# A decoder block's feed-forward part: rows for four operand sums fetched one part earlier, and half of one inner product's weight differences made in later products

## The chip, the cores and the metric

The kernel runs on one core of one Trainium2 chip. The metric is the device time of one execution in microseconds (us); the time of a version is the median of its runs. A profile shows one execution, with the busy time of each engine: PE (TensorE, the matrix multiplies), DVE (VectorE), ACT (ScalarE), POOL (GpSimd) and SP (SyncE, which here only issues DMAs, in the order of its own instruction list).

## The reference, cut to what matters

One decoder layer: a mixer of pooling and attention, then a feed-forward part with the square of a ReLU, in float32, 2048 rows, width 1024, inner width 4096. The change is in the feed-forward part alone (the last three lines before the final norm):

```python
h = h + einsum('bse,ed->bsd', mixed, w_out)
hn2 = rmsnorm(h, norm2_g)
up = einsum('bsd,df->bsf', hn2, w_up)
act = square(relu(up))
h = h + einsum('bsf,fd->bsd', act, w_down)
return rmsnorm(h, final_g)
```

## The kernel before

Every float32 operand is split into a high and a low part, and a product is done as three matmuls on 128x128 weights and 128x512 rows. The split takes one ACT copy (line L146) and one DVE subtract (L147). Products are arranged in the way of Strassen: a block product is seven smaller products P1 to P7 on sums and differences of operand blocks.

**up()** computes the first matrix product in 32 columns, numbered (q, m): q is the first or second half of the rows, m one of 16 column blocks of `w_up`. A column is its seven products, twelve matmuls each (L1082, into the accumulators pX, pY and pZ), so 84 matmuls. The scheduler that lays out the program sets the order of the instructions on each engine, and it may put products of neighbouring columns next to each other. After a product, `post` does the work on its result: after P7 a DVE add (L1032) reads the accumulator pZ, and the twelve matmuls of P3, which go on accumulating in that same pZ, wait for it. `post` also stores the sums (L1003), 256 KB each.

The second half of the rows (q = 1) needs sums of its own operand blocks. They are made by `sums_second(n, part)` for n = 0 to 3, during the columns q = 0, m = 2 to 5: part 0 at product P2 of the column, part 1 at P5, part 2 at P4. A part calls `normed_of(h, i)`, which loads a 256 KB row block `hn` from `hs` by SP (L955) and scales it in place on DVE (L956). Then follow the adds (L951) and the stores (L950). DVE works in the order of its list, so an instruction that waits for `hn` holds up all behind it.

**down()** computes the second matrix product in seven products, one after the other: P1, P6, P7, then P4, P5 and P2, each of which is itself done by seven inner products, and at last P3. A step of P1, P6 or P7 is 48 matmuls (L1422): one 512 KB weight block `wr` (loaded at L1142, split into `wd`) and two 512 KB row blocks `ar` (loaded from `sd` at L1197, split into `ad`), one for each half of the rows. The eight steps of a product take the blocks in the order `TURN` = 3, 7, 2, 6, 1, 5, 0, 4. An inner step of P4, P5 or P2 is 12 matmuls (L1249).

The inner products of P4, P5 and P2 need differences of weight blocks. `inner_weights(i, kk, t)` makes them from a pair of blocks kk and kk + 4: four DVE subtracts of 128x512 (L1137) and four 256 KB stores (L1138). For P2 this is done during P1: `more_weights` loads block `w_down[2, kk]` once more for each of the eight steps. That is eight loads, sixteen subtracts and sixteen stores.

Loads by SP go through one queue with eight completion semaphores used in turn. A load or a store on SP therefore waits for the eighth one before it.

Of the kernel before, what the change touches and what calls it, by code (L numbers as in the profile page):

```python
# [46 lines left out]
def hymba_block(ctx: ExitStack, tc: tile.TileContext, xT, gains, w_in, pool_w, w_out, w_up, w_down, out):  # L47
    nc = tc.nc
# [84 lines left out]
    hs = [dram.tile([KD, P, T], F32, name=f"hs{j}") for j in range(NT)]  # L133
# [685 lines left out]
    def root_last(i, ss, where=None, tag="px"):  # L819
        y = inv_root(mean_squares([ss], D, where, tag), nc.gpsimd)  # L820
        nc.gpsimd.tensor_copy(yrlast[:, i, 0], y)
        nc.gpsimd.tensor_tensor(yrlast[:, i, 1], y, yrlast[:, i, 0].bitcast(F32), ALU.subtract)
# [18 lines left out]
    A11, A12, A22, S1, S2, S3, S4 = range(7)  # L841
    PAIRS = ((0, 1), (3, 2))
# [18 lines left out]
    def up(pools, more):  # L861
# [3 lines left out]
        cols = [(q, m + x * (NM // 2)) for q in range(2) for m in range(NM // 2)[::(1, -1)[q]] for x in range(2)]  # L865
# [78 lines left out]
        SUMS, second = ("P2", "P5", "P4"), {}  # L944

        def sums_second(n, part):

            c, k = n // 2, n % 2
            new = lambda name: avp.tile([P, T], F32, tag="av", name=name)
            keep = lambda i, t: nc.sync.dma_start(su[1][i][c][:, k], t)  # L950
            add = lambda to, x, y, op: nc.vector.tensor_tensor(to, x, y, op)  # L951

            def normed_of(h, i):
                t, j = new("hn"), PAIRS[1][h]
                nc.sync.dma_start(t, hs[j][i])  # L955
                nc.vector.scalar_tensor_tensor(t, t, g2[:, i:i + 1], rlast[:, j - 2], op0=ALU.mult, op1=ALU.mult)  # L956
                return t

            if part == 0:
                second["a21"], a22 = normed_of(1, n), normed_of(1, 4 + n)  # L960
                second["s1"] = new("hs1")
                add(second["s1"], second["a21"], a22, ALU.add)
                keep(A22, a22)
                keep(S1, second["s1"])
            elif part == 1:
                a11, a21, s1 = normed_of(0, n), second["a21"], second["s1"]
                add(a21, a11, a21, ALU.subtract)
                second["s2"] = new("hs2")
                add(second["s2"], s1, a11, ALU.subtract)
                keep(A11, a11)  # L970
                keep(S3, a21)
                keep(S2, second["s2"])
            else:
                a12, s4 = normed_of(0, 4 + n), new("hs4")
                keep(A12, a12)
                add(s4, a12, second["s2"], ALU.subtract)
                keep(S4, s4)
# [90 lines left out]
        for g, (q, m, s) in enumerate(slots):  # L1068
            while lefts and lefts[0][0] <= g + LA:
                make_left(*lefts.pop(0)[1:])  # L1070
            if q == 0 and 2 <= m < 6 and s in SUMS:
                sums_second(m - 2, SUMS.index(s))
            if q == 0 and (m in (1, 6, 7) or m >= NM // 2 and m % (NM // 2) not in (2, 3, 4, 5)) and s in SUMS:
                next(first_weights, None)
            bank, first, last = what[s][2:]
            if first:
                ps[q, m, bank] = psu.tile([P, T], F32, tag=bank, name="p" + bank)
            t, w = ps[q, m, bank], ops.pop(g)
            for c in range(G):
                a = left_ops[q, s][c // 2]  # L1080
                for x, (wx, ax) in enumerate(((0, 0), (0, 1), (1, 0))):
                    nc.tensor.matmul(t, w[:, wx, c], a[:, ax, c % 2], start=first and c == 0 and x == 0,  # L1082
                                     stop=last and c == G - 1 and x == 2, skip_group_check=True)
            post(q, m, s)
            if g == 1:
                root_last(1, sslast, psu, "R")
            elif g in (6, 10):
                pr, i = psu.tile([P, T], F32, tag="R", name="pr"), g // 10
                spread(pr, yrlast[:, i])
                nc.scalar.activation(rlast[:, i], pr, AF.Copy)  # L1090
            if g + UA < len(slots):
                make_weights(g + UA)
                q2, m2, s2 = slots[g + UA]
                n = cols.index((q2, m2)) + 2
                if s2 == "P3" and n < 2 * NM:
                    load(*cols[n])

    def down(pools):
# [9 lines left out]
            else:  # L1108
                steps += [(n, i, kk, (0, 1)) for kk in range(8)]
        steps += [("P3", S4, kk, (q,)) for q in range(2) for kk in range(8)]  # L1110
        made, turns = {}, {"ar": -2, "ad": 0}

        def row(shape, kind, tag, **kw):
            early, late_ = {"ar": rs, "ad": s8}[tag]
# [14 lines left out]
        def inner_weights(i, kk, t):  # L1129

            if kk < 4:
                tops[i] = t
                return
            b, k = {(x, y): half(w, y) for x, w in enumerate((tops.pop(i), t)) for y in range(2)}, kk - 4
            for to, x, y, p in (((0, 0), (0, 1), (0, 0), "P5"), ((0, 1), (1, 1), (0, 1), "P7"),
                                ((1, 1), (1, 1), (0, 0), "P6"), ((1, 0), (1, 0), (1, 1), "P4")):
                nc.vector.tensor_tensor(b[to], b[x], b[y], ALU.subtract)  # L1137
                nc.sync.dma_start(wi[i][p][k // 2][:, 2 * (k % 2):2 * (k % 2) + 2], b[to])  # L1138

        def blk(i, kk, where=None):  # L1140
            t = (where or rt).tile([P, 4, 256], F32, tag="wr", name="wr")
            nc.sync.dma_start(t, w_down[i, kk] if isinstance(i, int) else td[int(i[1]) - 1][kk])  # L1142
            return t
# [4 lines left out]

        def more_weights(n, kk, w):

            if n == "P1":
                inner_weights(A12, kk, blk(2, kk))
            elif n == "P6":
                minus(blk(2, kk, rtx), w)
                nc.sync.dma_start(td[1][kk], w)
            elif n == "P7":
                inner_weights(A22, kk, blk("t2", kk))

        def make_inner(n, p, kk):

            i, kp = SPLIT[n], kk // 2
            if kk % 2 == 0:
                if p in wi[i]:
                    w = rt.tile([P, 4, 256], F32, tag="wr", name="wq")
                    nc.sync.dma_start(w, wi[i][p][kp])
                else:
                    w = quarter(source[n], kp, *{"P1": (0, 0), "P2": (1, 0), "P3": (1, 1)}[p])
                t = made["inner"] = t8.tile([P, 2, 4, 256], F32R, tag="wd", name="wd", align_bytes=256)
            r = row([P, 2, T], F32, "ar")
            nc.sync.dma_start(r, {"P1": sd[0][i][kk], "P2": sd[0][i][kk + 4], "P4": sd[1][i][kk + 4]}[p]  # L1170
                              if p in ("P1", "P2", "P4") else sdi[i][("P5", "P6", "P7", "P3").index(p)][kk])
            if kk % 2 == 0:
                split((t[:, 0], t[:, 1]), w)
            a = row([P, 2, 2, T], F32R, "ad", align_bytes=256)
            split((a[:, 0], a[:, 1]), r)
            return made["inner"], a

        def make(g):
            n, i, kk, qs_ = steps[g]
            if qs_ is None:  # L1180
                made[g] = make_inner(n, i, kk)
                return
            if n != "P3":
                kk = TURN[kk]
            b11, b12, b21, b22 = range(4)
            if n == "P1":
                w = blk(b11, kk)
            elif n == "P6":
                w = minus(blk(b22, kk), blk("t1", kk))
            elif n == "P7":  # L1190
                w = minus(blk(b22, kk), blk(b12, kk))
            else:
                w = blk(b22, kk)
            rows = {q: row([P, 2, T], F32, "ar") for q in qs_}
            for q in qs_:
                with tc.issue_after(last[0].ins) if n == "P1" and last[0] else nullcontext():
                    last[0] = nc.sync.dma_start(rows[q], sd[q][i][kk])  # L1197
            t = t8.tile([P, 2, 4, 256], F32R, tag="wd", name="wd", align_bytes=256)
            split((t[:, 0], t[:, 1]), w)
            left_ = {}  # L1200
            for q in qs_:
                left_[q] = row([P, 2, 2, T], F32R, "ad", align_bytes=256)
                last[1] = split((left_[q][:, 0], left_[q][:, 1]), rows[q])
            while late and n != "P1":
                late.pop(0)()
            late.append(lambda: more_weights(n, kk, w))
            made[g] = t, left_
# [200 lines left out]
        for g, (n_, i, kk, qs_) in enumerate(steps):  # L1408
            t, left_ = made.pop(g)
# [204 lines left out]
```

## Time and profile before

| | |
|---|---|
| median of 3 runs | 1913.87 us (1913.1 to 1915.24) |
| the profiled execution, its own time | 1917.71 us |
| its span, first to last instruction | 1915.9 us |
| PE busy in the span | 1891.8 us (99%) |
| up(), 2688 matmuls of 128x512 | about 698 to 1312 us |
| down(), products P1, P6, P7 (1152 matmuls) | 1312.12 to 1575.41 us |
| down(), products P4, P5, P2 (1008 matmuls) | 1575.41 to 1804.87 us |

Times inside the span count from its first instruction. A row of a timeline gives the start, the duration, the engine, the line of the kernel, the operation, the output and the input, how many instructions it stands for, and in brackets the idle time before it with what ended it. A run of twelve matmuls shows 2.88 us, of which the last part overlaps with the next run: the next one starts 2.72 us later. A row of the chain of waits gives a start, a duration and who held the chain then. In a table by windows each engine has its busy time (with its instructions in brackets), then come the granted clock, the share of the 16 DMA engines' time and the rate in GB/s.

### The profile page before, as it was taken

To read this page: it belongs to the slowest core of one execution; us is meant where nothing else is said; L and a number is where in the kernel's file an instruction comes from. 1 tells how busy PE (TensorE), PEld (TensorE's weight loads), DVE (VectorE), ACT (ScalarE), POOL (GpSimd) and SP (SyncE) were. 2 spreads that over 40 slices of the span, in tenths; PEclk is the share of its full clock that TensorE was granted. 3 is DMA by queue.
4 is the path that set the end of the run, shared out by engine and by line. 5 is a ranking of instruction groups with operands and counts; after the bars stand their busy time and mean duration, and the time that the engine had idled before them with its cause. 6 is when DMAs were issued, how large, how long until landed. Compare 5 with 4: busy or idle time off the path is not lost.

```text
span 1915.9 us, 26510 instructions
## 1 busy us (share of the span) xinstructions
PE 1891.8 (99%) x8995; PEld 1577.8 (82%) x8995; DVE 1424.4 (74%) x2128; ACT 1006.7 (53%) x1598; POOL 177.7 (9%) x399
## 2 busy tenths in 40 slices
PE   9999999999999999999999999999999999999997
PEld 7888888888888888788888888887888888888886
DVE  6887799667866886776787877786655547888874
ACT  5565566555554465455566555454333345656643
POOL 0211113101211030000000000000010010020120
PEclk9999999999999999999999999999999999999998
DMA  6686596787887867776777677778998889899862
GB/s 213 204 270 201 191 295 221 244 312 264 283 321 295 282 239 252 261 254 227 273 285 269 233 258 262 243 266 310 379 358 308 282 253 314 291 297 334 295 209 91
DMA packets 206034, 509.68 MB, mean 266 GB/s; under 512 B 24256, under 2 KB 30400, under 8 KB 202048
## 3 DMA queue, kind: packets, MB, share of 16 engines
q1 hardware_dynamic: 201136, 499.24, 75.1%
q0 software_dynamic: 4608, 8.39, 2.4%
q8 instruction: 73, 1.20, 0.3%
q14 instruction: 73, 0.60, 0.1%
q10 hardware_dynamic: 144, 0.26, 0.0%
HBM read 335.82 MB, written 171.97 MB: 265 GB/s over the span
## 4 chain that ended last, share of the span: by engine, by line
PE 89%; DMA 4%; DVE 4%; issue 1%; ACT 1%; POOL 0%; SPq 0%; DVEq 0%; ACTq 0%
PE pY L1082 16%; PE pb L1422 16%; PE pb L1249 12%; PE pZ L1082 8%; PE pd L178 8%; PE pd L180 8%; PE pd L179 8%; PE pX L1082 4%; PE po L675 2%; PE pta L664 1%; DMA xt<-in_xT_dram 1%; PE pr L231 1%; DMA t<-in_w_down_dram 1%; PE pm L205 1%; PE pz L617 1%; DMA wr<-in_w_down_dram 1%
## 5 line engine op out<-in xcount | busy, mean ns | idle before, releaser
L1082 PE MATMUL pY<-sa,hw 128*128 128x512 f32 x1536 | 365.7, 389 | 0.7 <-ACT u L1015 0.7
L1422 PE MATMUL pb<-ad,wd 128*128 128x512 f32 x1488 | 340.9, 390 | 1.3 <-ACT ad L146 1.2
L1082 PEld LDWEIGHTS pY<-sa,hw 128*128 128x128 f32 x1536 | 288.1, 188 | 60.9 <-ACT u L1015 1.1
L1422 PEld LDWEIGHTS pb<-ad,wd 128*128 128x128 f32 x1488 | 278.5, 188 | 60.0 <-ACT ad L146 1.6
L178 PE MATMUL pd<-h,hl 128*128 128x512 f32 x752 | 299.8, 399 | 0.7 <-DVE qkr L424 0.7
L180 PE MATMUL pd<-h,hl 128*128 128x512 f32 x752 | 296.9, 395 | 0.0
L179 PE MATMUL pd<-h,hl 128*128 128x512 f32 x752 | 296.7, 395 | 0.0
L147 DVE TENSOR_TENSOR ad<-ar,ad 128x1024 fp32r<-128x1024 f32 x148 | 179.8, 1221 | 70.2 <-ACT ad L146 70.0
L1249 PE MATMUL pb<-ad,wd 128*128 128x512 f32 x1008 | 229.2, 389 | 0.5 <-DVE ad L147 0.5
L1249 PEld LDWEIGHTS pb<-ad,wd 128*128 128x128 f32 x1008 | 189.0, 188 | 40.4 <-DVE ad L147 1.2
L146 ACT ACTIVATE ad<-ar 128x1024 fp32r<-128x1024 f32 x148 | 155.6, 1053 | 116.8 <-issue 47.6
L1082 PE MATMUL pZ<-sa,hw 128*128 128x512 f32 x768 | 186.7, 390 | 1.5 <-DVE a L1032 1.5
L1082 PEld LDWEIGHTS pZ<-sa,hw 128*128 128x128 f32 x768 | 143.9, 188 | 32.2 <-DVE a L1032 2.4
L178 PEld LDWEIGHTS pd<-h,hl 128*128 128x128 f32 x752 | 142.1, 189 | 28.2 <-DVE qkr L424 1.0
L180 PEld LDWEIGHTS pd<-h,hl 128*128 128x128 f32 x752 | 141.8, 189 | 28.0
L179 PEld LDWEIGHTS pd<-h,hl 128*128 128x128 f32 x752 | 142.0, 189 | 27.1
L146 ACT ACTIVATE hl<-raw 128x512 fp32r<-128x512 f32 x168 | 104.0, 631 | 111.2 <-PE pd L180 70.7
L147 DVE TENSOR_TENSOR hl<-raw,hl 128x512 fp32r<-128x512 f32 x168 | 114.1, 685 | 53.6 <-ACT hl L146 50.0
L147 DVE TENSOR_TENSOR hw<-rt,hw 128x512 fp32r<-128x512 f32 x128 | 86.8, 686 | 51.4 <-ACT hw L146 51.3
L1009 ACT ACTIVATE a<-a 128x512 f32<-128x512 f32 x96 | 59.5, 630 | 86.8 <-DVE a L1048 41.4
L146 ACT ACTIVATE wd<-wr 128x1024 fp32r<-128x1024 f32 x40 | 42.4, 1060 | 112.4 <-PE pb L1422 94.1
L1082 PE MATMUL pX<-sa,hw 128*128 128x512 f32 x384 | 93.1, 389 | 0.0
(219 smaller groups left out, 2652.2 us busy)
## 6 DMA issues: line engine op xcount, KB each, us to landing
ar<-sd SPq DMA_DIRECT2D x100, 512.0 KB, 5.4
wr<-in_w_down_dram SPq DMA_DIRECT2D x64, 512.0 KB, 5.4
rb<-in_w_up_dram SPq DMA_DIRECT2D x30, 1024.0 KB, 6.4
sd<-a SPq DMA_DIRECT2D x112, 256.0 KB, 4.0
raw<-in_w_in_dram SPq DMA_DIRECT2D x50, 512.0 KB, 4.5
ar<-sdi SPq DMA_DIRECT2D x48, 512.0 KB, 5.7
sd<-s SPq DMA_DIRECT2D x88, 256.0 KB, 4.0
sdi<-hr SPq DMA_DIRECT2D x72, 256.0 KB, 4.4
```

Source lines behind the costliest of these rows:

```text
L146: nc.scalar.activation(hi, src, AF.Copy)
L147: return nc.vector.tensor_tensor(lo, src, hi.bitcast(F32), ALU.subtract)
L178: nc.tensor.matmul(ps, hl[:, 0, c], hi, start=(k == 0), stop=False)
L179: nc.tensor.matmul(ps, hl[:, 0, c], lo, start=False, stop=False)
L180: mm = nc.tensor.matmul(ps, hl[:, 1, c], hi, start=False, stop=(k == n - 1))
L205: marks["pm"] = nc.tensor.matmul(pm[:, c:c + 1], ss[:, c * P:(c + 1) * P], inv[n], start=(i == 0), stop=(i == len(parts) - 1))
L231: mm = nc.tensor.matmul(pr[:, b * P:(b + 1) * P], yr[:, x, b:b + 1].to_broadcast([P, P]), identr, start=(b == 0 and x == 0), stop=(b == TB ...
L675: nc.tensor.matmul(po[:, p * 256 + to:p * 256 + to + hi - lo], vw[:, 2 * p + v], at[:, x, lo:hi], start=(p == 0 and n == 0 and x == 0), sk ...
L1009: nc.scalar.activation(t, src, AF.Relu)
L1082: nc.tensor.matmul(t, w[:, wx, c], a[:, ax, c % 2], start=first and c == 0 and x == 0, stop=last and c == G - 1 and x == 2, skip_group_che ...
L1249: nc.tensor.matmul(b, t[:, wx, 2 * (kk % 2) + c, i * P:(i + 1) * P], a[:, ax, c], start=p in ("P1", "P5", "P2") and kk == 0 and c == 0 and ...
L1422: nc.tensor.matmul(ps[q, n], block(t, wx, c, n), left_[q][:, ax, c], start=(n_ in ("P1", "P3") and kk == 0 and c == 0 and x == 0), stop=(n ...
```

## The change

Two edits, both in the feed-forward part.

The first splits the load of `hn` from its scaling. A new helper `fetch(h, i)` allocates the tile and issues the load, and `normed_of` takes the tile that was fetched. A part fetches for the next part: a new part -1, called at product P4 of the column before, fetches the two blocks of part 0; part 0 fetches the block of part 1; part 1 that of part 2. The sixteen loads are the same, each one part earlier.

The second makes the weight differences for P2 at two places. During P1 only the pairs (1, 5) and (0, 4) are made. The pair (3, 7) is loaded at the first step of P4's inner product P5 and made at its fourth step, the pair (2, 6) in the same way in P5's inner product P5. Four loads of 512 KB, eight subtracts and eight stores of 256 KB are moved; none is added or dropped.

```diff
+            def fetch(h, i):
+                t = second[h, i] = new("hn")
+                nc.sync.dma_start(t, hs[PAIRS[1][h]][i])
+
             def normed_of(h, i):
-                t, j = new("hn"), PAIRS[1][h]
-                nc.sync.dma_start(t, hs[j][i])
+                t, j = second.pop((h, i)), PAIRS[1][h]
                 nc.vector.scalar_tensor_tensor(t, t, g2[:, i:i + 1], rlast[:, j - 2], op0=ALU.mult, op1=ALU.mult)
                 return t
 
+            for at in (((1, n), (1, 4 + n)), ((0, n),), ((0, 4 + n),), ())[part + 1]:
+                fetch(*at)
+            if part == -1:
+                return
...
+            nxt = cols[cols.index((q, m)) + 1:][:1]
+            if s == "P4" and nxt and nxt[0][0] == 0 and 2 <= nxt[0][1] < 6:
+                sums_second(nxt[0][1] - 2, -1)
...
-        made, turns = {}, {"ar": -2, "ad": 0}
+        made, turns, extra = {}, {"ar": -2, "ad": 0}, []
...
-            if n == "P1":
+            if n == "P1" and kk % 4 < 2:
                 inner_weights(A12, kk, blk(2, kk))
...
             if qs_ is None:
+                at = {("P4", "P5"): 3, ("P5", "P5"): 2}.get((n, i))
+                if at is not None and kk == 0:
+                    extra[:] = [blk(2, at), blk(2, at + 4)]
+                elif at is not None and kk == 3:
+                    for k in range(2):
+                        inner_weights(A12, at + 4 * k, extra.pop(0))
```

The scheduler lays the instructions out anew, and their order changes at places that the diff does not touch. Lines of the changed kernel are 7 to 16 higher: L1032 becomes L1039, L956 becomes L959, L1142 becomes L1152, L1197 becomes L1213.

**The SP queue at the start of P1.** `ar<-sd_0_2` are the row blocks of the third step of P1; `wr` are weight blocks; `sd` and `sdi` on the left are stores of up()'s last results. Before:

```order
L1142 DMA wr<-in_w_down_dram 128x1024
L883 DMA sdi_3_0_469<-hr 128x512
L1142 DMA wr<-in_w_down_dram 128x1024
L1003 DMA sd_1_4_381<-a_13497 128x512
L883 DMA sdi_0_0_425<-a_13365 128x512
L883 DMA sdi_1_0_429<-hr 128x512
L1003 DMA sd_6_4_421<-s_13508 128x512
L883 DMA sdi_3_0_437<-hr 128x512
L1197 DMA ar<-sd_0_2_315 128x1024
L1197 DMA ar<-sd_0_2_371 128x1024
L1197 DMA ar<-sd_0_6_319 128x1024
```

The same place with the change:

```order
L1152 DMA wr<-in_w_down_dram 128x1024
L883 DMA sdi_3_0_469<-hr 128x512
L1152 DMA wr<-in_w_down_dram 128x1024
L1010 DMA sd_1_4_381<-a_13497 128x512
L1152 DMA wr<-in_w_down_dram 128x1024
L883 DMA sdi_0_0_425<-a_13365 128x512
L883 DMA sdi_1_0_429<-hr 128x512
L1010 DMA sd_6_4_421<-s_13508 128x512
L883 DMA sdi_3_0_437<-hr 128x512
L1152 DMA wr<-in_w_down_dram 128x1024 x3
L1213 DMA ar<-sd_0_2_315 128x1024
L1213 DMA ar<-sd_0_2_371 128x1024
```

The first two `wr` are the weights of the third and fourth step in both. Four more `wr`, the weights of the fifth to eighth step, now stand ahead of the row blocks of the third step; before, they came one by one behind the row blocks of the steps ahead of theirs.

**DVE in the first column that makes these sums** (q = 0, m = 2). Each list begins with the last add of the column before. Before:

```order
L1052 TENSOR_TENSOR s_8871<-a_8866,s_8846 128x512
L147 TENSOR_TENSOR hw<-rt,hw 128x512
L956 SCALAR_TENSOR_TENSOR hn<-hn,gains,rlast 128x512 x2
L147 TENSOR_TENSOR hw<-rt,hw 128x512
L951 TENSOR_TENSOR hs_8883<-hn 128x512
L1021 TENSOR_TENSOR a_8900<-pX,p_8815 128x512
L147 TENSOR_TENSOR hw<-rt,hw 128x512
L147 TENSOR_TENSOR hw<-rb,hw 128x512
L956 SCALAR_TENSOR_TENSOR hn<-hn,gains,rlast 128x512
L951 TENSOR_TENSOR hn<-hn 128x512
L951 TENSOR_TENSOR hs_8929<-hs_8883,hn 128x512
L1032 TENSOR_TENSOR a_8966<-pZ,u_8964 128x512
```

With the change:

```order
L1059 TENSOR_TENSOR s_8875<-a_8870,s_8850 128x512
L922 TENSOR_TENSOR rt<-rb,rt 128x512
L951 TENSOR_TENSOR hs_8885<-hn 128x512
L1028 TENSOR_TENSOR a_8902<-pX,p_8815 128x512
L147 TENSOR_TENSOR hw<-rt,hw 128x512
L959 SCALAR_TENSOR_TENSOR hn<-hn,gains,rlast 128x512 x2
L951 TENSOR_TENSOR hn<-hn 128x512
L951 TENSOR_TENSOR hs_8931<-hs_8885,hn 128x512
L1039 TENSOR_TENSOR a_8968<-pZ,u_8966 128x512
```

The first two blocks are now scaled in the column before; the third and the fourth, which were scaled one at a time, are scaled together where the first two were, and the add that P3 waits for stands right behind their sums.

**PE in the same column.** `pZ_8934` (changed: `pZ_8936`) is the accumulator that P3 goes on with; its matmuls on `sa_8202` and `sa_8207` are P3. Before:

```order
L1082 MATMUL pZ_9091<-sa_7903,hw_9027 128x512 x2
L1082 MATMUL pY_8979<-sa_7893,hw_8994 128x512 x6
L1082 MATMUL pY_8979<-sa_7898,hw_8994 128x512 x6
L1082 MATMUL pZ_9091<-sa_7903,hw_9027 128x512 x4
L1082 MATMUL pZ_9091<-sa_7908,hw_9027 128x512 x6
L1082 MATMUL pZ_8934<-sa_8202,hw_8947 128x512 x6
```

With the change:

```order
L1092 MATMUL pZ_9091<-sa_7903,hw_9027 128x512 x2
L1092 MATMUL pY_8981<-sa_7893,hw_8996 128x512 x6
L1092 MATMUL pY_8981<-sa_7898,hw_8996 128x512 x3
L1092 MATMUL pZ_8936<-sa_8202,hw_8949 128x512 x6
L1092 MATMUL pZ_8936<-sa_8207,hw_8949 128x512 x6
```

P3 stands 13 matmuls earlier: three of the product before it and all ten left of the next column's P5 have moved behind it.

## The prediction

> **What bounds the kernel now.** I read the busy times first, then what PE waited for, then the timeline at each of those waits.
>
> ```profile
> PE 1891.8 (99%) x8995; PEld 1577.8 (82%) x8995; DVE 1424.4 (74%) x2128; ACT 1006.7 (53%) x1598; POOL 177.7 (9%) x399
> ```
>
> PE is busy for 99% of the span, and neither edit adds or drops a matmul. So the time can change only by what PE waits for. From 700 to 1810 us, which holds everything that the change touches, the list of PE's waits has four rows (total, times, longest):
>
> ```profile
> PE pZ L1082 <- DVE a L1032: 1.5, 2, 1.2
> PE pb L1422 <- ACT ad L146: 1.2, 1, 1.2
> PE pY L1082 <- ACT u L1015: 0.7, 1, 0.7
> PE pb L1249 <- DVE ad L147: 0.5, 1, 0.5
> ```
>
> The first two are the ones that the edits can reach. The other two, and the smaller one of the two on L1032, are these:
>
> ```profile
> 779.51 3.02 PE L1082 MATMUL pZ<-sa,hw 128*128 128x512 f32 x12 [0.29 <-DVE a L1032]
> 1306.55 3.01 PE L1082 MATMUL pY<-sa,hw 128*128 128x512 f32 x12 [0.69 <-ACT u L1015]
> 1750.54 5.76 PE L1249 MATMUL pb<-ad,wd 128*128 128x512 f32 x24 [0.45 <-DVE ad L147]
> ```
>
> They lie before the first fetched row or far from any moved instruction (the last in P2's steps), and I leave them as they are. There is little to win: even if all four went, that would be 3.9 us as listed, some 5 us with the unlisted part found below. There is no such limit to what can be lost.
>
> **The first wait: column m = 2 of up().** PE's timeline, then DVE's:
>
> ```profile
> 798.69 2.88 PE L1082 MATMUL pY<-sa,hw 128*128 128x512 f32 x12
> 801.41 2.43 PE L1082 MATMUL pZ<-sa,hw 128*128 128x512 f32 x10
> 805.07 3.03 PE L1082 MATMUL pZ<-sa,hw 128*128 128x512 f32 x12 [1.23 <-DVE a L1032]
> ```
>
> ```profile
> 797.35 0.75 DVE L956 SCALAR_TENSOR_TENSOR hn<-hn,gains,rlast 128x512 f32<-128x512 f32 x1 [4.59 <-DMA hn<-hs]
> 798.25 0.75 DVE L956 SCALAR_TENSOR_TENSOR hn<-hn,gains,rlast 128x512 f32<-128x512 f32 x1
> 798.92 0.68 DVE L147 TENSOR_TENSOR hw<-rt,hw 128x512 fp32r<-128x512 f32 x1
> 802.33 0.75 DVE L956 SCALAR_TENSOR_TENSOR hn<-hn,gains,rlast 128x512 f32<-128x512 f32 x1 [0.32 <-DMA hn<-hs]
> 803.12 0.69 DVE L951 TENSOR_TENSOR hn<-hn 128x512 f32<-128x512 f32 x1
> 803.73 0.69 DVE L951 TENSOR_TENSOR hs<-hs,hn 128x512 f32<-128x512 f32 x1
> 804.33 0.68 DVE L1032 TENSOR_TENSOR a<-pZ,u 128x512 f32<-128x512 f32 x1
> ```
>
> Twelve matmuls take 2.72 us (798.69 to 801.41), one 0.227. The ten from 801.41 end at 803.68, and P3 starts at 805.07: 1.39 us lost. P3 waits for L1032, and L1032 stands behind the scaling of the third block, which landed only for 802.33.
>
> With the change the third and fourth blocks are loaded where the first two were, behind the same 1 MB load of `w_up`, so I let them land as those did: the scalings start at 797.35 and 798.25. The next instruction may follow 0.67 later (798.92); two adds take 0.61 and 0.60 (steps from 803.12 to 803.73 and 804.33); so the add for P3 starts at 800.13 and ends near 800.8 in place of 805.0. But P3 now stands 13 matmuls earlier and is due at 803.68 - 13 x 0.227 = 800.73. With the 0.06 us that PE took to start after L1032 (804.33 + 0.68 = 805.01, start 805.07), it starts at 800.87. What remains is 0.14, the gain **1.25 us**. It is bounded by 1.39 (nothing remains) and by 0.35, if the blocks land 0.9 us later than their predecessors did (the distance of the rows 797.35 and 798.25).
>
> The other three columns did not stall. There P3 is also put earlier, so the cover has to be checked; the tightest is m = 4:
>
> ```profile
> 871.05 0.75 DVE L956 SCALAR_TENSOR_TENSOR hn<-hn,gains,rlast 128x512 f32<-128x512 f32 x1 [4.39 <-DMA hn<-hs]
> 872.32 0.74 DVE L956 SCALAR_TENSOR_TENSOR hn<-hn,gains,rlast 128x512 f32<-128x512 f32 x1
> 878.66 5.60 PE L1082 MATMUL pZ<-sa,hw 128*128 128x512 f32 x24
> ```
>
> P3 is the second half of the last row, due at 878.66 + 2.72 = 881.38. The changed list has it 22 matmuls earlier: 876.39. The add for it would end near 872.32 + 0.67 + 0.61 + 0.60 + 0.68 = 874.9. That leaves 1.5 us of cover: cost 0, and if the blocks came 2 us later, 0.5. The first two blocks are now scaled in the column before, behind that column's own add for P3, and leave DVE the idle time that they had (4.59 and 4.39 above): 0.
>
> **The second wait: the third step of P1.** PE, then the chain of waits, then ACT:
>
> ```profile
> 1312.12 22.27 PE L1422 MATMUL pb<-ad,wd 128*128 128x512 f32 x96
> 1335.57 9.71 PE L1422 MATMUL pb<-ad,wd 128*128 128x512 f32 x40 [1.17 <-ACT ad L146]
> ```
>
> ```profile
> 1319.86 7.83 DMA wr<-in_w_down_dram
> 1327.71 6.72 DMA ar<-sd
> 1334.46 1.06 ACT ad L146
> 1335.55 1.24 DVE ad L147
> 1336.83 3.24 PE pb L1422 x13
> ```
>
> ```profile
> 1334.46 1.06 ACT L146 ACTIVATE ad<-ar 128x1024 fp32r<-128x1024 f32 x1 [3.70 <-DMA ar<-sd]
> 1335.73 1.06 ACT L146 ACTIVATE ad<-ar 128x1024 fp32r<-128x1024 f32 x1 [0.22 <-DMA ar<-sd]
> 1336.98 1.06 ACT L146 ACTIVATE ad<-ar 128x1024 fp32r<-128x1024 f32 x1 [0.19 <-DMA ar<-sd]
> ```
>
> The 96 matmuls from 1312.12 end at 1333.88, so step 3 starts 1.69 us late. Its rows `ar` were issued at 1327.71, at the moment when the weight load of 1319.86, the eighth DMA before them in the list, had landed (1327.69). They then took 6.72 us. Why so long is in the windows:
>
> ```profile
> 1312.00:1323.00 11.00, 11.00 (x51) 9.09 (x49) 8.71 (x13) 3.28 (x4) 0.00 (x0) 1.00 1.04 365
> 1323.00:1334.00 11.00, 10.95 (x48) 8.74 (x47) 3.67 (x3) 3.19 (x3) 0.00 (x0) 1.00 0.94 361
> 1345.00:1356.00 11.00, 11.00 (x51) 9.09 (x49) 8.70 (x10) 4.35 (x5) 0.00 (x0) 1.00 1.03 410
> ```
>
> The DMA engines are full (shares 1.04 and 0.94) from the start of P1. What is ahead of the rows in the queue is what delays them. In the changed list four weight loads of 512 KB, meant for steps 5 to 8, stand ahead of the rows of step 3, where before none of them did. This is the term against the change. The three ACT rows start 1.27 and 1.25 apart, each as its 512 KB have landed, so four such loads take 4 x 1.26 = **5.0 us**. Bounds: at 361 GB/s, the rate with up()'s stores in between, 2.10 MB take 5.8; if the free 6% of the slice from 1323 on (0.66 us of 11) are filled first, 4.4. The rows then land near 1339.5 and step 3 starts near 1340.6. ACT and DVE also have a weight split ahead of the rows that stood behind them; it can run when step 2 ends (1333.9), takes 1.06 + 1.24 us, and is done long before 1339.5: cost 0 under that wait, 1.1 if the wait were not there. Nothing gives the time back, as PE has no other idle time in P1.
>
> What the edit means to save, half of the extra weight loads, stands in P1 behind step 3, where PE did not wait: gain 0.
>
> The Trainium skill, page "DMA: Bandwidth & Descriptors", section "Where 436 GB/s comes from", holds that HBM limits a core to about 358 GB/s; an estimate by that makes the four loads 5.9 us and the sum 0.9 larger. The 410 GB/s of the window from 1345 on disagrees.
>
> **The moved weight differences in P4 and P5.** The scheduler puts the first four subtracts into the end of P7, the second four into the end of P4. The windows there, and the subtracts of P7 as a group:
>
> ```profile
> 1553.00:1564.00 11.00, 11.00 (x50) 9.13 (x49) 4.14 (x4) 3.07 (x3) 0.00 (x0) 1.00 0.97 335
> 1640.00:1651.00 11.00, 11.00 (x50) 9.11 (x49) 10.24 (x12) 8.12 (x10) 0.00 (x0) 1.00 0.87 277
> 1651.00:1662.00 11.00, 11.00 (x51) 9.09 (x49) 8.45 (x9) 6.67 (x7) 0.00 (x0) 1.00 0.90 303
> ```
>
> ```profile
> L1137 DVE TENSOR_TENSOR wr<-wr 128x512 f32<-128x512 f32 x16 | 11.0, 690 | 0.4
> ```
>
> Four subtracts of 0.69 are 2.8 us of DVE. In P7 DVE is busy 4.14 of 11, so 0. Around 1640 to 1662 it is busy 18.7 of 22, which leaves 3.3: it fits, barely. The two loads and four stores are 2.1 MB, 5 us at 410 GB/s, against a DMA share of 0.87 to 0.90. PE waited once, 0.5 us, in all 1008 matmuls of P4, P5 and P2, so operands are ahead of it. I take 0 and keep 2 us as the other bound: 2.8 that do not fit, less the 0.8 or so that the operands are ahead at least.
>
> **The sum.** -1.25 + 5.0 + 0 + 0 = **+3.75 us** on the profiled execution (1917.71 us, span 1915.9), which lies 3.8 above the median of the runs. The difference carries over to the median: 1913.87 + 3.75 = **1917.6 us**. With the bounds it is -1.39 + 4.4 = +3.0 at the least and -0.35 + 5.8 + 0.5 = +5.95 at the most: 1916.9 to 1919.8.
>
> **The rivals.**
>
> *Both waits go.* If the row blocks of step 3 profit from the smaller load in P1 instead of standing behind it, the 1.69 go as well as the 1.25: -2.9, 1911 us. For it: both waits are on the chain. Against it: the moved loads stood behind the rows of step 3, not ahead of them, so taking them out cannot make these earlier; four others came ahead. 7%.
>
> *The four loads do not delay the rows.* If the 16 DMA engines work on rows and weights at once and a later transfer can be done first, step 3 starts as before, and at most the weight split costs 1.1 us on ACT: -1.25 + (0 to 1.1), about 1912.9 us, no change to be told. Against it: the three row blocks landed one after the other, 1.26 apart. The Trainium skill, page "DMA: Bandwidth & Descriptors", section "Queues, rings and completion order", says that completion is not in the order of issue for one issuing engine, which speaks for this rival; the even spacing of the rows quoted speaks against it here. 10%.
>
> *The second four subtracts collide.* If the two loads land late in P5's first steps, the subtract that waits for them holds up the splits of PE's operands behind it on DVE: it decides from the point where the wait exceeds the 3.3 us that DVE has free, and costs up to 2: 1919.6 us. For it: DVE 10.24 of 11. Against it: the loads are issued three steps (8 us) ahead. 13%.
>
> **How the numbers follow.** A measurement of this kernel can tell about 0.2%, 3.8 us, from no change. My forecast, 70%, lies on that line, at 1916.9 to 1919.8 by its bounds; these reach further up than down, so I put 39 of the 70 above it and 31 below. Slower: 39 + 13 = 52%. Same: 31 + 10 = 41%. Faster: 7%. For 8 in 10 the range takes the forecast's own bounds, the collision and most of the case without delay: 1912.5 to 1920.0.
>
> **What would show it.** Right: L1039 in column m = 2 ends near 800.8 and the wait of pZ on it is below 0.4; four `wr` loads land between 1329 and 1340, and the wait of pb on ACT's `ad` at the third step of P1 grows from 1.2 to about 6; no wait over 0.5 in the inner products. Wrong: step 3 starting before 1337, which would make it the second rival; new waits of pZ in the columns m = 3 to 5; or a wait in P4 or P5 of over 1 us.

## The result, and the profile after

The changed kernel takes 1922.01 us (median of 6 runs, 1919.62 to 1925.17), the kernel before 1913.54 us beside it (6 runs, 1912.74 to 1915.24). The ratio is 1.0044, with an interval of 1.0031 to 1.0057: slower by 8.5 us. The forecast was 1917.6 us, with a range to 1920.0. Its direction holds, its size does not. One execution among the experiments, of the run with two loads ahead, took 2706.24 us at a mean granted clock of 0.65; it is left out of that run's median.

PE's waits from 700 to 1810 us in the changed kernel (total, times, longest):

```profile
PE pb L1438 <- ACT ad L146: 6.3, 1, 6.3
PE pY L1092 <- ACT u L1022: 1.6, 2, 0.8
PE pb L1265 <- DVE ad L147: 0.4, 1, 0.4
```

The wait of pZ on DVE's add is gone. The wait at the third step of P1 has grown from 1.2 to 6.3 us. PE's timeline there, and the starts of P4 and of P3:

```profile
1311.09 21.92 PE L1438 MATMUL pb<-ad,wd 128*128 128x512 f32 x96
1339.27 242.43 PE L1438 MATMUL pb<-ad,wd 128*128 128x512 f32 x1056 [6.26 <-ACT ad L146]
1581.54 174.75 PE L1265 MATMUL pb<-ad,wd 128*128 128x512 f32 x769
...
1811.04 5.60 PE L1438 MATMUL pb<-ad,wd 128*128 128x512 f32 x24
```

The two steps end at 1311.09 + 96 x 0.2267 = 1332.85, so step 3 starts 6.42 us late (1.69 before). The chain of waits shows why, as foreseen:

```profile
1320.99 8.46 DMA wr<-in_w_down_dram
1329.46 0.02 issue
1329.47 8.67 DMA ar<-sd
1338.14 0.02 issue
1338.16 1.06 ACT ad L146
1339.23 0.04 issue
1339.27 5.92 PE pb L1438 x13
```

The rows `ar` were issued when the eighth DMA before them had landed, now one of the four hoisted weight loads, and landed at 1338.14, which is 27.05 us after the start of P1. Before it was 22.32 (1334.44 - 1312.12). That is 4.7 us more, against 5.0 foreseen.

But the last row holds something that was not foreseen: 13 matmuls took 5.92 us; before, the 13 at this place took 3.24. The windows around it show the granted clock, the third number from the end:

```profile
1311.00:1333.00 22.00, 22.00 (x98) 17.89 (x96) 12.31 (x16) 6.47 (x7) 0.00 (x0) 1.00 1.03 383
1333.00:1335.00 2.00, 0.01 (x1) 0.00 (x0) 0.86 (x1) 1.06 (x1) 0.00 (x0) 1.00 1.01 410
1335.00:1339.00 4.00, 0.00 (x0) 0.00 (x0) 0.36 (x1) 0.84 (x1) 0.00 (x0) 0.50 1.03 413
1339.00:1345.00 6.00, 5.73 (x14) 4.49 (x15) 5.50 (x5) 4.45 (x5) 0.00 (x0) 0.50 0.82 276
1345.00:1349.00 4.00, 4.00 (x19) 3.32 (x18) 0.72 (x2) 1.06 (x1) 0.00 (x0) 0.97 0.90 327
```

PE had been idle for 2.15 us when its clock fell to half at 1335.0. It stayed there until 1345.24 (0.97 in the last slice is 0.24 us of half clock), 6 us into the work that had meanwhile begun. Those 6 us did the work of three: **3.0 us lost on top of the wait**. "PE busy" does not show it, since a slow matmul is as busy as a fast one. In the page's totals it can hardly be seen: PE has 2.7 us more of busy time for the same instructions (1891.8 before), but a second trace of the kernel before, below, has 1887.6. The page's row of the granted clock has a slice of 8 there, with 9 on both sides.

```profile
PE 1894.5 (99%) x8995; PEld 1580.0 (82%) x8995; DVE 1421.1 (74%) x2128; ACT 1007.0 (52%) x1598; POOL 179.4 (9%) x399
```

By stages, from the starts of their first matmuls, with a second trace of each kernel that was taken among the experiments (us):

| stage | before | before, second | changed | changed, second |
|---|---|---|---|---|
| start of up() | 696.97 | 692.32 | 696.22 | 693.63 |
| up() | 615.15 | 615.48 | 614.87 | 615.61 |
| P1, P6, P7 | 263.29 | 263.10 | 270.45 | 268.65 |
| P4, P5, P2 | 229.46 | 229.24 | 229.50 | 229.55 |
| P3 and the end | 111.03 | 111.06 | 111.06 | 110.86 |

Only P1 to P7 has changed, by 269.55 - 263.20 = 6.35 us on average. The ratio's interval is 5.9 to 10.9 us, so this is within it, at its lower end. What comes ahead of up() is untouched by the change and varies by 4.7 us between two executions of the same kernel; the 3.8 us by which the first profile of before stood above its median are of that kind. The clock can have a part in this too: in that stage it stood at 0.50 for 10.2 us in the first trace of before and never in the second. The pair of the changed kernel goes the other way (3.4 us with the start at 696.22, 6.8 us with the start at 693.63), so it is not the only one.

### The profile page after: what moved, and what is told of

It reads as the page before. It is cut to its first block, busy times and chain, and to the rows that moved or that the text cites. A ratio compares the mean times of both kernels' runs of the same rounds, so it can differ in the third digit from the quotient of the medians.

```text
span 1922.1 us, 26494 instructions
## 1 busy us (share of the span) xinstructions
PE 1894.5 (99%) x8995; PEld 1580.0 (82%) x8995; DVE 1421.1 (74%) x2128; ACT 1007.0 (52%) x1598; POOL 179.4 (9%) x399
## 4 chain that ended last, share of the span: by engine, by line
PE 91%; DVE 4%; DMA 3%; ACT 1%; issue 1%; POOL 0%; SPq 0%; DVEq 0%; ACTq 0%; POOLq 0%
PE pY L1092 17%; PE pb L1438 16%; PE pb L1265 12%; PE pd L178 8%; PE pd L180 8%; PE pd L179 8%; PE pZ L1092 8%; PE pX L1092 4%; PE po L675 2%; PE pta L664 1%; PE pr L231 1%; PE pm L205 1%; PE pz L617 1%; DMA wr<-in_w_down_dram 1%; PE pz L618 1%
```

## The experiments

Each run is compared with the kernel before on the same chip: 1913.37 us for the first four, 1913.56 for the next four, 1913.36 for the last three. The idle time ahead of step 3 is always the start of its first matmul less the start of P1 and 21.76 us (96 matmuls).

**The first edit alone** (`more_weights` and `make` as before).

> The first edit alone. Theory (the slowdown is the later rows of P1's third step plus the half clock that follows the long idle time): no slowdown, 0 to 1 us below the kernel before, since the wait at m = 2 goes (1.4 us) but is partly given back later in up(); third step of P1 1 to 2 us late as before, granted clock 1.00 there. Rival (the earlier loads cost something themselves): 1 us or more above the kernel before.

Measured: 1911.77 us, ratio 0.9992 (0.9983 to 1.0001). No slowdown; in its trace step 3 followed with no listed wait, where 1 to 2 us had been expected, at a clock of 1.00.

**The second edit alone** (`sums_second` as before).

> The second edit alone. Theory: the whole slowdown, 7 to 9 us above the kernel before; PE idle about 6 us at the third step of P1, granted clock 0.5 for 6 to 10 us around it. Rival (the two edits only cost together): less than 5 us above.

Measured: 1921.11 us, ratio 1.0043 (1.0030 to 1.0056), 7.7 us above. The second edit does it all. PE's timeline, then the windows:

```profile
1309.77 21.92 PE L1428 MATMUL pb<-ad,wd 128*128 128x512 f32 x96
1337.58 62.75 PE L1428 MATMUL pb<-ad,wd 128*128 128x512 f32 x269 [5.89 <-ACT ad L146]
```

```profile
1334.00:1340.00 6.00, 2.42 (x6) 1.94 (x7) 2.42 (x3) 3.09 (x3) 0.00 (x0) 0.50 1.02 404
1340.00:1341.00 1.00, 1.00 (x4) 0.77 (x3) 0.96 (x2) 0.72 (x2) 0.00 (x0) 0.59 0.89 320
```

Idle 6.05 us, half clock until 1340.82, so 3.24 us into the work, 1.6 us lost.

**Both edits, the rows first.** The weight loads of steps 5 to 8 are held behind the rows of the step before theirs:

```diff
             if n == "P1":
-                w = blk(b11, kk)
+                with tc.issue_after(last[0].ins) if TURN.index(kk) >= 4 else nullcontext():
+                    w = blk(b11, kk)
```

> Both edits, and the weight loads of steps 5 to 8 of P1 held behind the rows of the step before theirs. Theory: the slowdown is gone, 0 to 1.5 us below the kernel before; third step 1 to 2 us late, clock 1.00. Rival (the weight differences made in P4 and P5 cost 2 us or more, or the clock falls for another reason): still 2 us or more above the kernel before.

Measured: 1912.42 us, ratio 0.9997 (0.9988 to 1.0006). The slowdown is gone, with the weight differences still made in P4 and P5. Step 3 is 0.77 us late, less than expected.

```profile
1306.98 21.92 PE L1439 MATMUL pb<-ad,wd 128*128 128x512 f32 x96
1329.51 70.71 PE L1439 MATMUL pb<-ad,wd 128*128 128x512 f32 x309 [0.61 <-ACT ad L146]
```

**The changed kernel with PE kept busy.** 24 matmuls on zero weights fill the idle time; they add nothing to the sums, and one DVE copy makes the zeros.

```diff
+            if g == 1:
+                for x in range(24):
+                    nc.tensor.matmul(ps[1, 3], zeror, left_[1][:, 0, x % 2], start=False, stop=False,
+                                     skip_group_check=True)
```

> The changed kernel, with 24 matmuls on zero weights added behind the second step of P1, where PE would be idle; they add nothing to the sums, and one DVE copy makes the zeros. Theory: the rows come as late as in the changed kernel, but the granted clock stays 1.00, so 2 to 3.5 us below the changed kernel (some 4 to 6 above the kernel before), and the runs scatter less than the changed kernel's 5.5 us. Rival (the clock after the idle time costs nothing, the rest of the slowdown sits elsewhere): as the changed kernel, 8 us above the kernel before.

Measured: 1918.76 us, ratio 1.0033 (1.0022 to 1.0044), so 3.3 us below the changed kernel, although PE has more to do. The two ratio intervals overlap (1.0022 to 1.0044 here, 1.0031 to 1.0057 there), so the medians alone leave some doubt; the trace is clearer. Timeline and windows:

```profile
1331.07 5.75 PE L1448 MATMUL pb<-ad,zeror 128*128 128x512 f32 x24
1337.02 63.21 PE L1440 MATMUL pb<-ad,wd 128*128 128x512 f32 x276 [0.19 <-ACT ad L148]
```

```profile
1331.00:1337.00 6.00, 5.82 (x26) 4.36 (x24) 1.23 (x2) 2.12 (x2) 0.00 (x0) 1.00 1.03 410
1337.00:1345.00 8.00, 7.92 (x34) 6.25 (x35) 6.89 (x6) 5.32 (x5) 0.00 (x0) 1.00 0.92 320
```

Step 3 still starts 5.95 us after the end of step 2, with the rows as late as ever, but the clock stays at 1.00, and P1 to P7 take 267.55 us, against 270.45 and 268.65 in the two traces of the changed kernel. This takes the clock's part from the wait's. The expected smaller scatter did not come: the runs went from 1915.74 to 1923.45. So the scatter does not come from the clock at this place, or not mainly; the start of up() alone lies between 691.6 and 697.0 us in the traces of this study.

**One, two and three of the four loads ahead of the rows**: the hold from index 5, 6 and 7 of `TURN` on.

> As the run with the rows first (1912.4 us), but one of the four weight loads stands ahead of the rows of step 3. Theory (each load delays the rows by 1.26 us; the clock is halved only after an idle time of some 2 to 3 us or more): step 3 is 2 to 3 us late, granted clock 1.00, 1.3 us above the run with the rows first, 1913.7 us. Rival (a fixed loss as soon as the order changes): 3 us or more above it.

> Two of the four loads ahead of the rows. Theory: step 3 is 3 to 4.2 us late; that is around the length from which the clock falls, so 2.5 us above the run with the rows first plus up to 3: 1915 to 1918 us. Rival (stall alone, no clock): 1914.9 us with the clock at 1.00 or not.

> Three of the four loads ahead of the rows. Theory: step 3 is 4.4 to 5.5 us late and the clock is 0.5 for 6 to 10 us around the restart: 3.8 us for the stall and 1.7 to 3.4 for the clock above the run with the rows first, 1918 to 1919.6 us. Rival (stall alone): 1916.2 us.

Timelines of the three, in this order:

```profile
1314.02 21.92 PE L1439 MATMUL pb<-ad,wd 128*128 128x512 f32 x96
1338.75 61.44 PE L1439 MATMUL pb<-ad,wd 128*128 128x512 f32 x263 [2.82 <-ACT ad L146]
```

```profile
1306.84 21.92 PE L1439 MATMUL pb<-ad,wd 128*128 128x512 f32 x96
1331.81 68.48 PE L1439 MATMUL pb<-ad,wd 128*128 128x512 f32 x289 [3.06 <-ACT ad L146]
```

```profile
1311.04 21.92 PE L1439 MATMUL pb<-ad,wd 128*128 128x512 f32 x96
1336.65 63.59 PE L1439 MATMUL pb<-ad,wd 128*128 128x512 f32 x267 [3.68 <-ACT ad L146]
```

With the others, ordered by idle time. The medians are of all runs of a kernel; the columns from "idle" on are of one execution each, which took 1921.94, 1916.23 and 1921.38 us with one, two and three loads ahead. "Half clock" is the time at 0.50, summed over windows of 1 us; "lost by it" is half of its part after the restart of PE. Without any loss P1 to P7 would be 1152 x 0.2267 = 261.1 us; the last two columns are to be compared.

| loads ahead | median, ratio (interval) | idle | half clock | lost by it | 261.1 + idle + lost | P1 to P7 |
|---|---|---|---|---|---|---|
| 0, rows first | 1912.42, 0.9997 (0.9988 to 1.0006) | 0.77 | 0 | 0 | 261.9 | 262.40 |
| 0, before (second trace) | 1913.5, 1 | 1.48 | 0 | 0 | 262.6 | 263.10 |
| 1 | 1914.56, 1.0005 (0.9997 to 1.0014) | 2.97 | 3.4 | 1.6 | 265.7 | 265.76 |
| 2 | 1915.39, 1.0015 (1.0006 to 1.0024) | 3.21 | 6.8 | 2.9 | 267.2 | 267.14 |
| 3 | 1918.65, 1.0024 (1.0014 to 1.0034) | 3.85 | 6.8 | 2.9 | 267.9 | 267.87 |
| 4 (second trace) | 1922.01, 1.0044 (1.0031 to 1.0057) | 5.64 | 6.8 | 1.9 | 268.6 | 268.65 |
| 4, second edit alone | 1921.11, 1.0043 (1.0030 to 1.0056) | 6.05 | 6.8 | 1.6 | 268.8 | 268.79 |
| 4 (first trace) | as above | 6.42 | 10.2 | 3.0 | 270.5 | 270.45 |

The two terms account for every trace to within 0.5 us. The expectation that one load ahead leaves the clock at 1.00 missed: 2.97 us of idle time brought it down. That of 4.4 to 5.5 us idle with three loads missed too: the loads do not add 1.26 us each in single traces, as the landing of the rows varies by about a microsecond. With two loads ahead the half clock cost nearly as much (2.9 us) as the idle time that caused it (3.2).

**Second traces of both kernels**, for the table of stages.

> The kernel before once more, for a second trace. Theory (its first trace had a slow first stage, up() from 696.97 us on, and a wait at the third step of P1 at the long end): up() starts earlier, 692 to 696 us; up() itself again takes 615 us; the idle time ahead of the third step of P1 is 0 to 1.7 us with the clock at 1.00, P1 to P7 262 to 263.3 us. Rival (the difference of 8.5 us in the medians has a source that the stages do not show): stages as in the first trace.

> The changed kernel once more, for a second trace. Theory (free windows of the clock): the idle time ahead of step 3 is again 5.5 to 6.5 us, the granted clock falls to 0.5 at some point of it and comes back within 7 us of the restart, but at other distances from the restart than before; P1 to P7 268.5 to 271 us, P4 to P2 229 to 230 us. Rival (part of the loss sits elsewhere): P1 to P7 below 268 us or another stage longer.

Measured: 1913.02 and 1920.22 us, one run each. PE's timelines, before and changed, and the window of the changed kernel in which the clock came back:

```profile
1307.80 21.92 PE L1422 MATMUL pb<-ad,wd 128*128 128x512 f32 x96
1331.04 69.33 PE L1422 MATMUL pb<-ad,wd 128*128 128x512 f32 x303 [1.32 <-ACT ad L146]
```

```profile
1309.24 21.92 PE L1438 MATMUL pb<-ad,wd 128*128 128x512 f32 x96
1336.64 63.70 PE L1438 MATMUL pb<-ad,wd 128*128 128x512 f32 x272 [5.48 <-ACT ad L146]
```

```profile
1340.00:1341.00 1.00, 1.00 (x5) 0.76 (x4) 0.90 (x2) 0.79 (x2) 0.00 (x0) 0.82 1.07 344
```

Here the clock is back 3.7 us after the restart, in the first trace after 6 us: 1.9 and 3.0 us lost by the same program.

**The rows earlier still**: the hold from index 3, so that the weights of step 4 also come behind the rows of step 3; once with the first edit alone, once with both.

> The first edit alone, and the weights of step 4 of P1 held behind the rows of step 3, so that these rows come 1.26 us earlier. All weight differences for P2 are made in P1 as before. Theory: no wait of step 3 is left (0.6 to 1.7 us), so 0.5 to 1.5 us below the first edit alone: 1910.3 to 1911.3 us, 2 to 3 below the kernel before. Rival (the freed time is taken up by a later wait in P1, as in up()): as the first edit alone, 1911.8 us.

> Both edits, with the weights of step 4 and later of P1 each held behind the rows of the step before. Theory: step 3 does not wait; the weight differences in P4 and P5 cost and bring nothing, so as the first edit alone with the same hold, 1911.3 us. Rival (taking four loads and eight stores out of P1 brings something once the rows are first): 1 us or more below that.

Measured: 1911.32 us, ratio 0.9985 (0.9976 to 0.9994), and 1911.22 us, ratio 0.9985 (0.9975 to 0.9996). Neither has a wait in P1. From 690 to 1810 us PE has with both edits only two listed waits, of 1.6 us together, both on ACT's copy L1022 in up().

P1 to P7 take 261.23 and 261.12 us, which is no loss at all. These two beat both kernels, by 2 us or so: a real gain by their intervals, and less than the 0.2% that the prediction set as the line. How much of it is the hold's is not shown: the interval of the first edit alone (0.9983 to 1.0001) overlaps with both. Moving the weight differences into P4 and P5 brings nothing beside it.

## Why the prediction was wrong

**The loads ahead of the rows: right.** Its term was 5.0 us. The idle time ahead of step 3 grew by 6.42 - 1.69 = 4.7 in the first pair of traces and by 5.64 - 1.48 = 4.2 in the second. Holding the loads back (the rows first) removed the whole slowdown, so this is its cause, the part of the clock below included. The rival by which both waits go has fallen with that, and so has the one by which the four loads delay nothing. The bound from above, at 361 GB/s, was not needed: with loads alone in the queue the windows show 410 to 413.

**"Rows land near 1339.5 and step 3 starts near 1340.6", and from there as before: this step failed.** The sum priced a longer idle time of PE as that idle time and no more. It is missing the clock: 3.0 and 1.9 us in the two traces of the changed kernel, and 3.3 us between the medians when PE was kept busy. The idle time foreseen, 1.69 + 5.0, was in the prediction, but what it does to the clock was put at nothing without being named. From 700 to 1810 us, where the prediction looked, no row of the trace of before showed it: the longest idle time there, 1.7 us, left the clock at 1.00. Outside that stretch the same trace did show it. PE waited 2.52 us, and soon after its matmuls stood 0.43 us apart in place of 0.23:

```profile
457.73 0.39 PE L179 MATMUL pd<-h,hl 128*128 128x512 f32 x1
460.64 0.33 PE L231 MATMUL pr<-identr,yr 128*128 128x128 f32 x1 [2.52 <-DVE pc L629]
462.44 0.63 PE L178 MATMUL pd<-h,hl 128*128 128x512 f32 x1
462.87 0.63 PE L179 MATMUL pd<-h,hl 128*128 128x512 f32 x1
```

```profile
463.00:465.00 2.00, 2.00 (x6) 1.52 (x5) 2.00 (x4) 0.03 (x1) 0.00 (x0) 0.50 0.96 304
```

The clock stood at 0.50 for 3.41 us there, all of it under work, which makes the loss an estimated 1.7 us; with that term the sum would have been 1919.3. The second trace of before has the same wait of 2.52 us and no half clock after it, so the price is not always paid. The Trainium skill, page "TensorE: Matmul & The Clock Gate", section "Part 1: The HAM clock gate", says that TensorE runs at half clock after an idle window of about 3.4 us and that the window runs free of the program. The traces agree with half clock (0.50) and with the window: the stretches at 0.50 last 3.4, 6.8 and 10.2 us, one, two and three times 3.41. They differ in the length of idle time that suffices, below. An estimate from that page, half of one to two windows, is 1.7 to 3.4 us; with it the sum would have been 1919 to 1921.

**"The gain 1.25 us" at m = 2: shown where it was placed, not seen in up() as a whole.** DVE and PE of the changed kernel there:

```profile
796.25 1.41 DVE L959 SCALAR_TENSOR_TENSOR hn<-hn,gains,rlast 128x512 f32<-128x512 f32 x2 [3.23 <-DMA hn<-hs]
797.58 0.69 DVE L951 TENSOR_TENSOR hn<-hn 128x512 f32<-128x512 f32 x1
798.18 0.68 DVE L951 TENSOR_TENSOR hs<-hs,hn 128x512 f32<-128x512 f32 x1
798.78 0.68 DVE L1039 TENSOR_TENSOR a<-pZ,u 128x512 f32<-128x512 f32 x1
```

```profile
797.61 2.21 PE L1092 MATMUL pY<-sa,hw 128*128 128x512 f32 x9
799.65 2.91 PE L1092 MATMUL pZ<-sa,hw 128*128 128x512 f32 x12
```

The add ends 0.2 us before PE needs it, and P3 starts without a wait. In the three traces without the first edit that wait is listed with 1.23, 0.63 and 1.60 us; in those of the changed kernel it is gone. But up() as a whole takes 615.15, 615.48 and 615.20 us without the first edit, and 614.8 (median of ten traces, 613.6 to 618.6) with it. The 0.4 us between them are less than this spread can tell. PE has new waits for an ACT copy (L1022) in place of the old one: 0.2 to 0.6 us near 793 us in seven of the ten traces with the first edit, and 0.7 to 1.9 us near 1004 us, where the second half of the rows begins, in six. Each of the ten has at least one of them, none of the three without the edit has either. In the first trace of the changed kernel the chain near 1004 us is:

```profile
999.28 3.90 DMA sr<-su
...
1003.54 0.16 ACT sa L146
1003.70 0.81 issue
1004.50 0.59 ACT u L1022
1005.09 0.04 issue
1005.13 0.97 PE pY L1092 x3
```

ACT waits for a row block of that half and has the copy that PE needs behind it. The longest of these waits, with one load ahead, cost more than itself. The twelve matmuls behind it took 4.48 us in place of 2.88:

```profile
1006.25 4.48 PE L1092 MATMUL pY<-sa,hw 128*128 128x512 f32 x12 [1.92 <-ACT u L1022]
```

The clock stood at 0.50 from 1007.5 to 1010.9 us there, and this up() is the one of 618.6 us. That the first gain is given back at these waits fits the traces; it was not tried by moving a load, and stays open. The run of the first edit alone (ratio 0.9983 to 1.0001) leaves room for 3 us of gain and for none.

**The moved weight differences: 0, as taken.** P4 to P2 take 229.5 us in all four traces to within 0.3. The rival of the collision, 13%, has fallen.

**The range and the chances.** Slower was given 52%, and came. The range ended at 1920.0 because the forecast's own bounds held only queue rates and landing times. The stages explain 6.35 of the 8.5 us between the medians; the other 2 are within the ratio's interval and were not found in any stage. Every sign that the prediction named for being right came: the add ended at 799.46 us with no wait of PE on it, the wait at step 3 was 6.3 us, and none in the inner products was over 0.5. These signs tested the waits, and none of them tested the clock.

## What to carry to other kernels

A wait of PE that grows past some two microseconds can have a second price: the clock was halved and stayed so for 3 to 6 us of the work after it. The sum needs a term for it even where the clock is at 1.00 in the whole stretch that the change touches; the rest of the same trace may show its size, as it did here. When an edit takes loads out of a full queue, look at what moves up into the room: here later weights were loaded early, ahead of rows that were needed at once, and holding them behind the rows cost one line. That they moved up because their buffers came free is likely and was not tried. And a gain of a microsecond early in a stage that is fed by DMA may be no gain when the loads after it do not come earlier too.

## What the runs showed of the hardware that was not expected

At step 3 of P1 the clock of TensorE fell in six traces, 2.1 to 2.9 us after PE's last matmul (2.1 in the first trace of the changed kernel, 2.9 with three loads ahead), which is less than a whole window of 3.41 us. It came back 3.2 to 6.0 us after PE had begun again, and the time at half clock was always a multiple of that window. Within each trace all changes of the clock lie whole multiples of 3.41 us apart, also those in different stages (in the first trace of before at 8.22, 15.04, 462.19 and 465.60 us).

The length of the idle time alone does not decide. In up() and P1 the shortest one that brought the clock down was 2.09 us (with one load ahead, listed as 1.92 near 1004 us), and the longest that left it at 1.00 was 1.76 us (the run of the second edit alone, listed as 1.60 at 802.73 us). Ahead of up(), 2.52 us brought it down in one trace of before and not in the other, and with two loads ahead it was down for 3.41 us from 446.67 us on, behind a listed idle time of only 1.27 us. Where an idle time lies against these multiples may be the reason; no run here set it.

Matmuls on zero weights were enough to keep the clock at 1.00.
